# One hybrid layer on one core: the last plain tiles of the up projection are turned into Strassen steps

## The chip, the cores and the metric

The kernel runs on one core of one Trainium2 chip. The time is device time of one execution in microseconds; it is measured in several executions, and the median is given. A core has five engines with a queue each that is worked through strictly in order: TensorE (PE, with PEld for its weight loads), VectorE (DVE), ScalarE (ACT), GpSimd (POOL) and SyncE (SP). SP's queue only issues transfers between HBM and the on-chip memory. POOL's queue issues transfers too: here those that add what they bring to what is already there. An engine that waits for one instruction also holds back all that stand behind it.

## The reference

One layer of an encoder for 512 positions of width 1024, in float32. A recurrent group and an attention group are mixed into the residual stream; then follows the part that this change touches, the feed-forward block with 4096 hidden units:

```python
x = x + mix @ w_out[l]
h = rms_norm(x, mlp_norm_g[l])
x = x + jnp.square(jax.nn.relu(h @ w_up[l])) @ w_down[l]
return rms_norm(x, final_norm_g)
```

`h @ w_up` is a product of 512x1024 by 1024x4096, `... @ w_down` one of 512x4096 by 4096x1024. The row scale of the norm is applied after the down projection (relu squared lets a positive scale through as its square), so what the up projection reads is `x1n` turned on its side and scaled by the norm's gain, called `h2`.

## The kernel before

**Precision.** TensorE works on a rounded 32-bit type. So every operand is split into a high part (a rounded copy, made by ACT) and a low part (what the copy lost, made by DVE), and each product is three matmuls: high by high, high by low, low by high (`mm3`, lines 312 to 314). For a weight chunk of 128x1024 (512 KB) these parts are `whi` (`conv_hi`, line 247) and `wlo` (`conv_lo`, line 269). The chunks of the whole kernel stand in one list, `chunks`; while a step works on chunk c, its hook `feed` converts chunk c+3: ACT after the third of eight products, DVE after the fifth. There are four buffers each of `whi` and `wlo`, three of raw chunks (`wraw`) and four of chunks that are being summed (`tw`).

**The up projection** runs in two halves of 16 tiles of 128 hidden units. A plain tile (`n0` to `n3`) is 8 x 3 matmuls of 512 columns. Four tiles together, named by the first of them (0, 4, 8, 12), can instead be taken as a 2x2 block product in Strassen's way, with seven products in place of eight: the steps `11`, `t1`, `21`, `t2`, `22`, `t3`, `t4`, each 8 x 3 matmuls of 256 columns. A step multiplies a combination of weight blocks by a combination of quarters of `h2`. The weights of `11`, `21` and `22` are blocks as they lie in HBM, loaded into `wraw`. Those of the others are sums in `tw` buffers: t1 = 12+11, t2 = t1+22, t4 = t2+21, t3 = 12+22. A step converts its chunk, and then the same buffer becomes the next sum. The four sums of `h2` that belong to the steps t1, t2, t3 and 22 (`hsum`) are made by `h_sums`, split into `hh` and `hl`, and also written to HBM (`hsd`) for the second half. The `h2` quarters themselves come from eight transposes of four 128x128 blocks each (`h2_t`): TensorE turns `x1n` into `pxt`, ACT copies it out twice (`h2h`, the high part, and `hm`, the whole), DVE subtracts (`h2l`, by `h2_l`). The first four can be made while the output projection still runs; the other four need the last `x1n`.

The second half has always been four Strassen groups. The first half consists of the plain tiles 0 to 3 and the groups 4, 8 and 12. The plain tiles n0, n1 and n2 are the head: they take turns over the eight quarters of `h2`, and the transposes for quarters 4 to 7 stand in one piece after the first three products.

**Down projection.** After each half its 16 tiles go through the down projection, seven products of four chunks each (`dmm`), a step every 2.7 us of TensorE time. Its weights are loaded ahead, four of them (`ts`) with an add on POOL's queue.

**What sets the order.** ACT, DVE, POOL and TensorE run in the order in which the program is written. Extra work is hung on a place in it by the table `late`: (group, step, product) to a function. SP's queue is ordered by a scheduler, except in some stretches, where it too goes by the program.

Of the kernel before, what the change touches and what calls it, by code (L numbers as in the profile page):

```python
# [44 lines left out]
for _n, _w in (("w0", 4), ("w1", 4), ("w2", 4), ("w3", 4), ("cb", 4),  # L45
# [9 lines left out]
    "n0 n1 n2 4:11 4:t1 n3 4:t2 4:21 4:22 4:t3 8:11 8:t1 4:t4 8:21 8:t2 8:22 8:t3 12:11 12:t1 8:t4 12:t2 12:22 12:t3 12:21 12:t4",  # L55
    "0:11 0:t1 0:21 0:t2 0:22 0:t3 8:11 8:t1 0:t4 8:21 8:t2 8:22 8:t3 12:11 12:t1 8:t4 12:21 12:t2 12:22 12:t3 4:11 4:t1 12:t4 4:t2 4:22 4:t3 4:21 4:t4")
QUADS = ((4, 8, 12), (0, 8, 12, 4))
ON_ACT = {(h, f, k) for h in range(2) for f in QUADS[h] if (h, f) != (0, 4) for k in ("21", "22", "t3", "t4")}

# [5 lines left out]
def up_steps(h):  # L65
    return [("n", int(s[1:])) if s[0] == "n" else (s.split(":")[1], int(s.split(":")[0])) for s in STEPS[h].split()]
# [32 lines left out]
def hybrid_kernel(ctx: ExitStack, tc, xw0, xw, xn, w_in, w_v, w_out, w_up, w_dn, gates, vecs, bias, fg, out):  # L99
# [90 lines left out]
    cu, cq, cd_ = {}, {}, []  # L190
    for h in range(2):
        for kind, f0 in up_steps(h):
            if kind == "n":
                cu[h, f0] = len(chunks)
                chunks.append(w_up[h * HF + f0])
            else:
                cq[h, f0, kind] = len(chunks)
                chunks.append((h, kind, f0, "u"))
# [37 lines left out]
    for (h, f0, kind), i in cq.items():  # L236
        if kind == "11" and (h, f0) != (0, 4):
            swap[i], swap[i + 1] = i + 1, i
# [22 lines left out]
    def conv_lo(i):  # L261
        if i < len(chunks):
# [11 lines left out]
            if isinstance(c, tuple) and len(c) == 4:  # L274
# [4 lines left out]
                elif kind == "22":  # L279
                    t = raws[cq[h, f0, "t3"]]  # L280
                    nc.vector.tensor_tensor(t, t, r, op=OP.add)
                elif kind in ("t2", "21"):
# [896 lines left out]
    def load_t(half, n, f0):  # L1179
        t = work.tile([P, 1024], FT, name="tw", tag="tw", bufs=4)  # L1180
        nc.sync.dma_start(t, ublock(half, "12", f0))
        for b in {"t1": ("11",), "t2": ("11", "22"), "t3": ()}[n]:
            nc.gpsimd.dma_start(t, ublock(half, b, f0), accum_op=OP.add)
        raws[cq[half, f0, n]] = t

# [64 lines left out]
    BES["s1"].update({1: lambda: (o_lo("22", 0), o_lo("22", 1), h2_t(0, "gs")), 2: lambda: h2_t(1, "gs"), 3: lambda: (conv_lo(C_WA + 8), h2_l(0))})  # L1250
    BES["22"].update({1: lambda: (h2_t(2, "gs"), h2_l(1)), 2: lambda: (h2_t(3, "gs"), conv_lo(C_WA + 9)), 3: lambda: (h2_l(2), h2_l(3))})
    for w in OSEQ:
# [7 lines left out]
        if w in ("s3", "s4", "21"):  # L1260
            load_t(0, {"s3": "t1", "s4": "t2", "21": "t3"}[w], 4)
# [20 lines left out]

    def h2k(k):
        return (h2h[:, k, :], h2l[k])
# [29 lines left out]
    def up_evac(ff, p):  # L1314
        q, c = ff // 2, slice((ff % 2) * TH, (ff % 2 + 1) * TH)
        for t in range(2):
            if (q, t) not in rb:
                rb[q, t] = g_("a")
            act(rb[q, t][:, c], p[:, t * TH:(t + 1) * TH], AF.Relu)
        if ff % 2:  # L1320
            for t in range(2):
                nc.vector.tensor_tensor(rb[q, t], rb[q, t], rb[q, t], op=OP.mult)
                rb_done.add((q, t))
            up_pair(q)


# [5 lines left out]
    def h_sums(k):  # L1332
        m, c = k // 2, slice((k % 2) * TH, (k % 2 + 1) * TH)
        if k % 2 == 0:
            for n in SUMS:
                hsum[n, m] = g_("hsum")
        a, b = hm.pop(k), hm.pop(k + 4)
        e, s2, s3, s4 = [hsum[n, m][:, c] for n in SUMS]
        nc.vector.tensor_tensor(e, b[:, right], a[:, right], op=OP.subtract)
        stt(s2, a[:, left], -1.0, e, op0=OP.mult, op1=OP.subtract)  # L1340
        nc.vector.tensor_tensor(s3, a[:, left], a[:, right], op=OP.subtract)
        stt(s4, b[:, left], -1.0, s2, op0=OP.mult, op1=OP.subtract)
        if k % 2:
            for i, n in enumerate(SUMS):
                nc.sync.dma_start(hsd[i][:, m * S:(m + 1) * S], hsum[n, m])

    HSEQ = [(n, m) for n in ("t1", "t2", "22", "t3") for m in range(2)]
    HJ = 20
    FGP = ((0, 32, 64, 128), (0, 32, 64, 96, 128))
# [150 lines left out]
    def load_s1(half, ts, qs=range(NQ)):  # L1500
        for q in qs:
            t = ts[:, q, :]
            nc.sync.dma_start(t, wblock(half, "11", q))
            nc.gpsimd.dma_start(t, wblock(half, "12", q), accum_op=OP.add)
            raws[cd_[half] + 2 * q + 1] = t
# [9 lines left out]
    for half in range(2):  # L1515
        c0, cd = cu.get((half, 0)), cd_[half]
# [4 lines left out]
        start = 0  # L1521
        if half == 0:
            start = 3
            pu = [ps_("pu", "pj") for _ in range(start)]
            for k in range(KD):
                if k == 1:
                    for j in range(4, 8):
                        h2_t(j, "gs" if j < 6 else "et")
                        h2_l(j)
                for i in range(start):  # L1530
                    mm3(pu[i], wk(c0 + i, k), h2k(k), k == 0, k == KD - 1)
                    if i == 0:
                        feed(c0, k)
                if k in (2, 3, 4, 5):
                    h_sums(k - 2)
                if k == 6:
                    x1_sq(0, 0)
# [272 lines left out]
```

## Time and profile before

| | |
|---|---|
| median of 3 runs | 525.56 us (525.28 to 526.11) |
| profiled execution | 525.8 us, its span 524.0 us |
| up projection, first half | 200.78 to 284.87 us of the span |
| PE busy | 517.3 us (99%) |
| DVE, ACT, POOL busy | 430.3, 351.9, 65.8 us |
| DMA | 105.15 MB, mean 201 GB/s |

The page of the profile gives busy times, a picture of the span in 40 slices, the transfer queues, the chain of work that ended last and the costliest groups of instructions. Groups, waits and timelines can be had for a stretch of the span. "Busy" of a matmul counts its whole pipelined life, so matmuls overlap in it; how fast they follow one another is read from their start times. The three runs span 0.16%, so a change of about 0.2% is what a measurement can tell.

### The profile page before, as it was taken

How to read it: one execution, taken by the hardware profiler on the slowest of the kernel's cores; microseconds unless marked ns; L12 is line 12 of the kernel's file. 1: busy time of each engine (PE TensorE's matmuls, PEld its weight loads, DVE VectorE, ACT ScalarE, POOL GpSimd, SP SyncE). 2: the span in 40 equal slices, each digit the busy share in tenths (PEclk: the TensorE clock that was granted, in tenths of full speed). 3: DMA queues.
4: the chain of work that ended last, by engine and by line, in shares of the span. 5: the costliest groups of instructions: out<-in, count | busy, mean ns of one | idle time of the engine just before them, and what ended most of it. 6: DMA issues, size and time to landing. Idle time of an engine off the chain costs nothing.

```text
span 524.0 us, 8211 instructions
## 1 busy us (share of the span) xinstructions
PE 517.3 (99%) x3021; PEld 444.0 (85%) x3021; DVE 430.3 (82%) x668; ACT 351.9 (67%) x568; POOL 65.8 (13%) x90
## 2 busy tenths in 40 slices
PE   9999999999999999999999999999999999999995
PEld 8867888778787788899999888889999999888884
DVE  6899986788886898898789987789766978986985
ACT  7579946667855848585578666565667577655664
POOL 0173000000000321001300311001101300140000
PEclk9999999999999999999999999999999999999999
DMA  8636545367696499847595899976977497799804
GB/s 288 213 98 198 160 155 180 91 182 206 185 286 218 102 194 275 326 129 196 136 225 144 217 273 275 309 268 161 295 235 194 116 226 208 154 286 256 201 1 161
DMA packets 40329, 105.15 MB, mean 201 GB/s; under 512 B 5056, under 2 KB 13376, under 8 KB 40288
## 3 DMA queue, kind: packets, MB, share of 16 engines
q1 hardware_dynamic: 32448, 78.10, 44.7%
q0 software_dynamic: 7696, 26.32, 27.1%
q8 instruction: 24, 0.39, 0.3%
q10 hardware_dynamic: 144, 0.20, 0.1%
q14 instruction: 17, 0.14, 0.1%
HBM read 95.59 MB, written 4.29 MB: 191 GB/s over the span
## 4 chain that ended last, share of the span: by engine, by line
PE 96%; issue 2%; DVE 1%; POOL 1%; DVEq 0%; ACT 0%; POOLq 0%; ACTq 0%
PE pu L313 10%; PE pu L312 10%; PE pu L314 10%; PE pd L312 10%; PE pd L313 10%; PE pd L314 10%; PE pqk L312 3%; PE pqk L314 3%; PE pqk L313 3%; PE pwo L312 2%; PE pt L842 2%; PE pwo L314 2%; PE pwo L313 2%; PE ps L806 2%; PE pav L942 2%
## 5 line engine op out<-in xcount | busy, mean ns | idle before, releaser
L269 DVE TENSOR_TENSOR wlo<-wraw,whi 128x1024 fp32r<-128x1024 f32 x71 | 86.6, 1221 | 23.1 <-ACT whi L247 22.9
L247 ACT ACTIVATE whi<-wraw 128x1024 fp32r<-128x1024 f32 x67 | 70.8, 1058 | 37.5 <-PE pd L314 18.2
L313 PE MATMUL pd<-wlo,ah 128*128 128x512 f32 (+1 forms) x195 | 75.2, 386 | 0.0
L312 PE MATMUL pd<-whi,ah 128*128 128x512 f32 (+1 forms) x195 | 75.2, 386 | 0.0
L314 PE MATMUL pd<-whi,al 128*128 128x512 f32 (+1 forms) x195 | 75.2, 386 | 0.0
L314 PE MATMUL pu<-hh,wlo 128*128 128x256 f32 x224 | 63.4, 283 | 0.0
L313 PE MATMUL pu<-hl,whi 128*128 128x256 f32 x224 | 63.4, 283 | 0.0
L312 PE MATMUL pu<-hh,whi 128*128 128x256 f32 x224 | 63.4, 283 | 0.0
L269 DVE TENSOR_TENSOR wlo<-tw,whi 128x1024 fp32r<-128x1024 f32 x37 | 45.2, 1221 | 18.1 <-ACT whi L247 18.1
L312 PE MATMUL pu<-h2h,whi 128*128 128x256 f32 (+1 forms) x200 | 60.1, 300 | 0.0
L313 PE MATMUL pu<-h2l,whi 128*128 128x256 f32 (+1 forms) x200 | 60.0, 300 | 0.0
L314 PE MATMUL pu<-h2h,wlo 128*128 128x256 f32 (+1 forms) x200 | 60.0, 300 | 0.0
L247 ACT ACTIVATE whi<-tw 128x1024 fp32r<-128x1024 f32 x38 | 40.1, 1059 | 26.3 <-PE pd L314 6.3
L247 ACT ACTIVATE whi<-ts 128x1024 fp32r<-128x1024 f32 x24 | 25.5, 1061 | 26.3 <-PE pd L314 18.3
L312 PEld LDWEIGHTS pu<-hh,whi 128*128 128x128 f32 x224 | 43.0, 192 | 0.0
L313 PEld LDWEIGHTS pu<-hl,whi 128*128 128x128 f32 x224 | 43.0, 192 | 0.0
L314 PEld LDWEIGHTS pu<-hh,wlo 128*128 128x128 f32 x224 | 43.0, 192 | 0.0
L314 PEld LDWEIGHTS pd<-whi,al 128*128 128x128 f32 x195 | 36.6, 188 | 7.4
L312 PEld LDWEIGHTS pd<-whi,ah 128*128 128x128 f32 x195 | 36.6, 188 | 7.3
L313 PEld LDWEIGHTS pd<-wlo,ah 128*128 128x128 f32 x195 | 36.6, 188 | 7.3
L312 PEld LDWEIGHTS pu<-h2h,whi 128*128 128x128 f32 x200 | 38.3, 191 | 1.3
L314 PEld LDWEIGHTS pu<-h2h,wlo 128*128 128x128 f32 x200 | 38.3, 191 | 1.3
(277 smaller groups left out, 1219.8 us busy)
## 6 DMA issues: line engine op xcount, KB each, us to landing
wraw<-in_w_up_dram SPq DMA_DIRECT2D x25, 512.0 KB, 4.4
ts<-in_w_dn_dram POOLq DMA_DIRECT2D x24, 512.0 KB, 13.3
wraw<-in_w_dn_dram SPq DMA_DIRECT2D x24, 512.0 KB, 9.2
tw<-in_w_up_dram SPq DMA_DIRECT2D x15, 512.0 KB, 5.1
tw<-in_w_up_dram POOLq DMA_DIRECT2D x15, 512.0 KB, 8.3
wraw<-in_w_in_dram SPq DMA_DIRECT2D x13, 512.0 KB, 3.8
ts<-in_w_dn_dram SPq DMA_DIRECT2D x8, 512.0 KB, 6.8
tw<-in_w_dn_dram SPq DMA_DIRECT2D x8, 512.0 KB, 7.3
```

The costliest lines, as they stand in the source:

```text
L247: act(hi, raws[i], AF.Copy)
L269: nc.vector.tensor_tensor(lo, r, f(splits[i][0]), op=OP.subtract)
L312: nc.tensor.matmul(o, lhsT=a[0], rhs=b[0], start=bool(first), stop=False, skip_group_check=on)
L313: nc.tensor.matmul(o, lhsT=a[0], rhs=b[1], start=False, stop=False, skip_group_check=on)
L314: nc.tensor.matmul(o, lhsT=a[1], rhs=b[0], start=False, stop=bool(last), skip_group_check=on)
L806: nc.tensor.matmul(psq[p, u][e][:, :NK], lhsT=qs_[p, a][r, P * qt:P * qt + P], rhs=kks[p][r, b, w:w + NK], start=i == 0, stop=i == 2)
L842: nc.tensor.transpose(pt[:, i * P:(i + 1) * P], en[h][qt][:, k:k + P], ident)
L942: nc.tensor.matmul(pav[p][a, co], lhsT=vs[:, jt, h * DH:(h + 1) * DH], rhs=et[h, jt][:, ci], start=jt == 0 and i == 0, stop=jt == 3 and i ...
```

## The change

- The tiles 0 to 3 of the first half become a Strassen group too. The first half is now 28 steps: `0:11 8:11 4:11 0:21 8:21 4:21 0:t1 8:t1 0:t2 0:22 0:t3 8:t2 8:22 4:t1 0:t4 8:t3 4:t2 8:t4 4:22 12:11 4:t3 12:t1 4:t4 12:t2 12:22 12:t3 12:21 12:t4`.
- In the first step, 0:11, all products that read the high part of `h2` come first, those with the low part last. The transposes of quarters 4 and 5 stand in the middle of this step, those of 6 and 7 in the next one.
- The sums of `h2` are made one by one, ahead of their step (`h_sum`). Those for t1 and t2 stay with DVE. Those for t3 (four instructions) and for 22 (eight) go to POOL.
- More of the weight sums are made by adding transfers on POOL's queue: t3 of group 0, and t4 of all four groups, which DVE added before. t2 of group 0 is a load with two adds. DVE still adds t3 of groups 8, 4 and 12. The `21` results wait for a later step to be taken out of PSUM (`put`).
- Six of the eight row sums of squares (`x1_sq`) move into the down projection's first steps. One of seven small loads of the final gain at the end falls away.
- The squares of all groups are now ACT's (`ON_ACT`).
- From the ninth step on SP's queue of this half goes by the program. The first of the `ts` loads is issued in step 18 (8:t4), the load and the add of t1 of group 4 come in steps 5 and 6, and its step stands behind 8:22.

```diff
-    "n0 n1 n2 4:11 4:t1 n3 4:t2 4:21 4:22 4:t3 8:11 8:t1 4:t4 8:21 8:t2 8:22 8:t3 12:11 12:t1 8:t4 12:t2 12:22 12:t3 12:21 12:t4",
+    "0:11 8:11 4:11 0:21 8:21 4:21 0:t1 8:t1 0:t2 0:22 0:t3 8:t2 8:22 4:t1 0:t4 8:t3 4:t2 8:t4 4:22 12:11 4:t3 12:t1 4:t4 12:t2 12:22 12:t3 12:21 12:t4",
...
+AJ = {(0, 4), (1, 0)}
+ADDED = {(0, 0), (0, 12)}
+RAW = {(0, 0), (0, 4), (0, 8), (0, 12)}
+ON_ACT = {(h, f, k) for h in range(2) for f in QUADS[h] for k in ("21", "22", "t3", "t4")}
...
+                elif (h, f0) in RAW and kind == "t2":
+                    nc.gpsimd.dma_start(r, ublock(h, "21", f0), accum_op=OP.add)
+                    raws[cq[h, f0, "t4"]] = r
...
-        a, b = hm.pop(k), hm.pop(k + 4)
-        e, s2, s3, s4 = [hsum[n, m][:, c] for n in SUMS]
-        nc.vector.tensor_tensor(e, b[:, right], a[:, right], op=OP.subtract)
-        stt(s2, a[:, left], -1.0, e, op0=OP.mult, op1=OP.subtract)
-        nc.vector.tensor_tensor(s3, a[:, left], a[:, right], op=OP.subtract)
-        stt(s4, b[:, left], -1.0, s2, op0=OP.mult, op1=OP.subtract)
...
+        if n == "t1":
+            nc.vector.tensor_tensor(o, b[:, right], a[:, right], op=OP.subtract)
+        elif n == "t2":
+            stt(o, a[:, left], -1.0, hsr["t1", m][:, c], op0=OP.mult, op1=OP.subtract)
+        elif n == "t3":
+            nc.gpsimd.tensor_tensor(o, a[:, left], a[:, right], op=OP.subtract)
+        else:
+            nc.gpsimd.tensor_tensor(o, a[:, left], b[:, left], op=OP.subtract)
+            nc.gpsimd.tensor_tensor(o, o, hsr["t1", m][:, c], op=OP.add)
...
+                if head:
+                    nc.tensor.matmul(o, lhsT=w[0], rhs=x[0], start=first, stop=False, skip_group_check=True)
+                    nc.tensor.matmul(o, lhsT=w[1], rhs=x[0], start=False, stop=False, skip_group_check=True)
+                    for m in range(8) if n == 7 else ():
+                        nc.tensor.matmul(bank[b][:, m // 4 * TH:(m // 4 + 1) * TH], lhsT=hi[:, m * P:(m + 1) * P], rhs=h_part(kind, m % 4)[1],
...
+                         (0, "11", 1): sums(*[("t3", k) for k in range(4)]), (8, "11", 0): sums(("t1", 0), ("t1", 1)), (8, "11", 5): split_h("t1", 0),
+                         (4, "11", 0): sums(("t1", 2), ("t1", 3), ("22", 0), ("22", 1), ("22", 2), ("22", 3)),
+                         (4, "11", 1): split_h("t1", 1), (0, "21", 0): sums(("t2", 0), ("t2", 1)),
...
+            if half == 0 and j < 6:
+                x1_sq(1 + j // 2, j % 2)
```

The rest of the table `late`, which places the loads, adds and splits, is left out. How the order of instructions moves at the places that matter is shown for three queues. The line numbers of the changed kernel are up to 13 higher.

POOL, from the adds into the first `tw` sums (12+11 and so on) onward. Before:

```order
L1183 DMA tw<-in_w_up_dram 128x1024 x4
L277 DMA tw<-in_w_up_dram 128x1024
L1183 DMA tw<-in_w_up_dram 128x1024
L277 DMA tw<-in_w_up_dram 128x1024
L1504 DMA ts<-in_w_dn_dram 128x1024 x4
```

and after:

```order
L1196 DMA tw<-in_w_up_dram 128x1024 x4
L1338 TENSOR_TENSOR hsum<-hm 128x256 x4
L1196 DMA tw<-in_w_up_dram 128x1024
L1340 TENSOR_TENSOR hsum<-hm 128x256
L1341 TENSOR_TENSOR hsum<-hsum 128x256
L1340 TENSOR_TENSOR hsum<-hm 128x256
L1341 TENSOR_TENSOR hsum<-hsum 128x256
L1340 TENSOR_TENSOR hsum<-hm 128x256
L1341 TENSOR_TENSOR hsum<-hsum 128x256
L1340 TENSOR_TENSOR hsum<-hm 128x256
L1341 TENSOR_TENSOR hsum<-hsum 128x256
L278 DMA tw<-in_w_up_dram 128x1024
```

Twelve subtractions and additions of 128x256 stand between the adds now; in all there are 14 adds of up weights in this half, where there were 7.

DVE, from the last row block of the output projection (`x1n`) to the conversion of 4:21, the last `wlo` of the piece. After:

```order
L1218 SCALAR_TENSOR_TENSOR x1n<-pwo,nrc,x_1559 128x512
L270 TENSOR_TENSOR wlo<-wraw,whi 128x1024 x3
L1234 TENSOR_TENSOR h2l<-hm,h2h 128x512 x2
L1334 TENSOR_TENSOR hsum<-hm 128x256 x2
L1234 TENSOR_TENSOR h2l<-hm,h2h 128x512 x2
L270 TENSOR_TENSOR wlo<-wraw,whi 128x1024
L1362 TENSOR_TENSOR hl<-hsum,hh 128x512
L1334 TENSOR_TENSOR hsum<-hm 128x256 x2
L1362 TENSOR_TENSOR hl<-hsum,hh 128x512
L270 TENSOR_TENSOR wlo<-wraw,whi 128x1024
```

Before, from the same `x1n` on:

```order
L1206 SCALAR_TENSOR_TENSOR x1n<-pwo,nrc,x_1559 128x512
L1222 TENSOR_TENSOR h2l<-hm,h2h 128x512 x6
L1339 TENSOR_TENSOR hsum<-hm 128x256
L1340 SCALAR_TENSOR_TENSOR hsum<-hm,hsum 128x256
L1341 TENSOR_TENSOR hsum<-hm 128x256
L1342 SCALAR_TENSOR_TENSOR hsum<-hm,hsum 128x256
```

Five conversions of weights (8:11, 4:11, 0:21, 8:21, 4:21) now stand among the head's sums, where before none came until eight sums were made.

SP, behind the first loads of up weights; `hsd` are the writes of the sums to HBM. After:

```order
L1189 DMA tw<-in_w_up_dram 128x1024 x2
L229 DMA wraw<-in_w_up_dram 128x1024
L1343 DMA hsd_2266<-hsum 128x512 x2
L229 DMA wraw<-in_w_up_dram 128x1024 x3
L1343 DMA hsd_2264<-hsum 128x512
L229 DMA wraw<-in_w_up_dram 128x1024
```

Before:

```order
L1181 DMA tw<-in_w_up_dram 128x1024 x2
L230 DMA wraw<-in_w_up_dram 128x1024 x3
L1503 DMA ts<-in_w_dn_dram 128x1024 x4
L1345 DMA hsd_2269<-hsum 128x512
L1345 DMA hsd_2270<-hsum 128x512
```

The loads of 8:21, 4:21 and 0:22 (the three in a row) stand behind two writes that wait for POOL's first four sums; the four `ts` loads are gone from this place.

More of the change, by code (lines that the diff above doesn't have):

```diff
@@ L1312, in hybrid_kernel @@
     rb_done = set()
[L1314 to L1324, printed above, removed]
     SUMS = ("t1", "t2", "t3", "22")
@@ L1498, in fin_other, with load_s1, add_s1 @@
         nc.vector.tensor_tensor(xf[tt], x1n[tt, 1], fgt[1], op=OP.mult)
[L1500 to L1505, printed above, removed]
+    def load_s1(half, ts, q):
+        nc.sync.dma_start(ts[:, q, :], wblock(half, "11", q))
+    def add_s1(half, ts, q):
+        t = raws[cd_[half] + 2 * q + 1] = ts[:, q, :]
+        nc.gpsimd.dma_start(t, wblock(half, "12", q), accum_op=OP.add)
     def load_s3(half, q):
@@ L1515, in hybrid_kernel @@
     for half in range(2):
[L1516 removed]
+        cd = cd_[half]
         rb_done.clear()
@@ L1617, in hybrid_kernel @@
         qs = QUADS[half]
-        for f0, f1 in zip(qs, qs[1:]):
+        for f0, f1 in zip(qs, qs[1:]) if half else ():
             late[f0, "t2", 0] = lambda f1=f1: load_t(half, "t1", f1)
@@ L1702, in hybrid_kernel @@
                 load_s3(half, q)
+            if half == 0 and j < 4:
+                nr2[j] = consts.tile([P, 1], FT, name="nr2_%d" % j)
+            if half == 0 and j < 6:
+                x1_sq(1 + j // 2, j % 2)
+            if half == 0 and j == 6:
+                for tt in range(4):
+                    nc.vector.tensor_scalar(nr2[tt], r2[tt], -1.0, None, op0=OP.mult)
             if half == 0 and j == 16:
```

169 lines of the change are left out of this document (80 added, 89 removed).

## The prediction

> **What bounds the kernel now.** I read the page's busy times first.
>
> ```profile
> PE 517.3 (99%) x3021; PEld 444.0 (85%) x3021; DVE 430.3 (82%) x668; ACT 351.9 (67%) x568; POOL 65.8 (13%) x90
> ```
>
> TensorE is the bound: busy in 99% of the span. In the table by stage, the head (201 to 230 us), the Strassen groups (230 to 285) and the down projection (285 to 362) show no gap of it and the full clock (1.00):
>
> ```profile
> 201.00:230.00 29.00, 29.00 (x160) 25.13 (x159) 25.13 (x44) 19.96 (x37) 0.00 (x0) 1.00 0.81 274
> 230.00:285.00 55.00, 55.00 (x459) 54.96 (x458) 46.29 (x65) 36.38 (x54) 6.93 (x8) 1.00 0.67 167
> 285.00:362.00 77.00, 77.00 (x345) 63.88 (x344) 65.61 (x81) 48.52 (x64) 12.10 (x14) 1.00 0.92 252
> ```
>
> (Columns: stretch, its length, busy PE, PEld, DVE, ACT, POOL, each with its count, then clock, DMA share, GB/s.) So time can be won only by giving TensorE less to do, and is lost wherever it begins to wait. What it has to do is read from start times in its timeline:
>
> ```profile
> 200.78 0.40 PE L312 MATMUL pu<-h2h,whi 128*128 128x512 f32 x1
> ...
> 202.84 1.95 PE L1216 MATMUL pxt<-ident,x1n 128*128 128x128 f32 x16
> 204.54 0.48 PE L312 MATMUL pu<-h2h,whi 128*128 128x512 f32 x1
> ...
> 224.69 0.40 PE L312 MATMUL pu<-h2h,whi 128*128 128x512 f32 x1
> ...
> 230.15 0.28 PE L312 MATMUL pu<-hh,whi 128*128 128x256 f32 x1
> ...
> 233.03 0.28 PE L312 MATMUL pu<-h2h,whi 128*128 128x256 f32 x1
> ...
> 284.87 0.40 PE L312 MATMUL pd<-whi,ah 128*128 128x512 f32 x1
> ```
>
> A plain tile (n3) takes 230.15 - 224.69 = 5.46 us, a Strassen step (4:t2) 233.03 - 230.15 = 2.88, that is 0.12 per matmul; the 16 transposes take 204.54 - 202.84 = 1.70.
>
> **The change, part by part.**
>
> *TensorE.* Four plain tiles go (4 x 5.46 = 21.84), seven steps come (7 x 2.88 = 20.16): -1.7 us. The transposes stay, split in two. The first step only has its products in another order. Counting steps from 1, step n now starts at 200.78 + 1.70 + 2.88 (n - 1) from the third on: 4:21, the sixth, at 216.9.
>
> *Work of DVE and ACT over the whole stage.* These rows give the prices:
>
> ```profile
> L1222 DVE TENSOR_TENSOR h2l<-hm,h2h 128x512 fp32r<-128x512 f32 x7 | 4.7, 689 | 2.1 <-ACT hm L1219 2.1
> L269 DVE TENSOR_TENSOR wlo<-wraw,whi 128x1024 fp32r<-128x1024 f32 x2 | 2.4, 1220 | 0.0
> L1339 DVE TENSOR_TENSOR hsum<-hm 128x256 f32<-128x256 f32 x4 | 1.7, 418 | 0.0
> L1206 DVE SCALAR_TENSOR_TENSOR x1n<-pwo,nrc,x 128x512 f32<-128x512 f32 x2 | 1.5, 745 | 0.0
> L1363 DVE TENSOR_TENSOR hl<-hsum,hh 128x512 fp32r<-128x512 f32 x2 | 1.3, 688 | 0.0
> L286 DVE TENSOR_TENSOR tw<-tw,wraw 128x1024 f32<-128x1024 f32 x7 | 8.6, 1223 | 0.1
> ```
>
> ```profile
> L247 ACT ACTIVATE whi<-wraw 128x1024 fp32r<-128x1024 f32 x13 | 13.9, 1071 | 2.3 <-PE pu L313 1.6 <-ACT scr L1271 0.7
> L1219 ACT ACTIVATE hm<-pxt,vt 128x512 f32<-128x512 f32 x8 | 5.6, 701 | 0.0
> L1379 ACT ACTIVATE v<-pu 128x512 f32<-128x512 f32 x9 | 5.5, 606 | 6.3 <-PE pu L314 6.3
> L1360 ACT ACTIVATE hh<-hsum 128x512 fp32r<-128x512 f32 x8 | 5.3, 662 | 4.4 <-DVE hsum L1339 4.4
> L1271 ACT ACTIVATE scr<-x1n 128x512 f32<-128x512 f32 x8 | 5.0, 630 | 0.0
> ```
>
> DVE gets three conversions more (3 x 1.22) and three result sums (3 x 0.69), and loses three weight sums (3 x 1.22), eight of sixteen `h2` sums (8 x 0.42) and seven squares of plain tiles and group 4 (7 x 0.69): about 6 us less. ACT gets about 6 more: three `whi`, three copies `v`, the squares of groups 0 and 4, less the relus of the plain tiles and six sums of squares (0.83 each with their read). Both then have some 63 to 66 us of work in 82, so on the whole stage they hide: nothing. The six sums of squares go beside the down projection, where ACT has 48.5 of 77 us: nothing.
>
> *The head is where the cover is thin.* Before, three interleaved plain tiles gave DVE and ACT 16 us before a fourth chunk was needed. Now a chunk is needed every 2.88 us from the start. I walk DVE's queue to 4:21, its tightest place; neighbours overlap by 0.08. With POOL at no cost: transposes 4 and 5 at 202.5, the last `x1n` ready at 202.2, low part of 8:11 until 203.4. Only then is a buffer free for 8:21. Its load goes behind two writes of sums; a like load took 7.1 us in this stretch:
>
> ```profile
> wraw<-in_w_up_dram SPq DMA_DIRECT2D x3, 512.0 KB, 7.1
> ```
>
> It lands at 210.5, so its high part is ready at 211.6 and its low part at 212.8. DVE was done with the rest at about 209, so it waited. Then: `hl` of t1 until 213.4, two sums until 214.1, ACT's `hh` 214.7 and `whi` of 4:21 215.75, DVE's `wlo` 217.0. TensorE wants it with the third product of the step, 216.9 + 0.24 = 217.1. So it is just in time, and what POOL does decides.
>
> *POOL's twelve sums.* No row shows a 128x256 sum on POOL. The nearest:
>
> ```profile
> L163 POOL TENSOR_TENSOR pl<-pl,z 128x8 f32<-128x8 f32 x8 | 3.7, 463 | 0.7
> masks.py:199 POOL TENSOR_SCALAR_AFFINE_SELECT ident<-ident 128x128 f32<-128x128 f32 x1 | 0.3, 291 | 0.1
> L136 POOL MEMSET mhalf<- 128x4 f32 x1 | 0.1, 100 | 0.0
> ```
>
> An operation over 128 columns takes 0.29 with about 0.1 of it fixed (the fill of four columns takes that): 0.48 for 256. And DVE and POOL keep each other waiting. While DVE reads PSUM, a tiny POOL sum takes 0.20; while it subtracts two on-chip tiles, one takes 1.09 and ends as that subtraction ends:
>
> ```profile
> 29.58 0.20 POOL L163 TENSOR_TENSOR pl<-pl,z 128x8 f32<-128x8 f32 x1
> ```
>
> ```profile
> 29.36 1.28 DVE L496 TENSOR_TENSOR xr<-pxr,rrow 128x512 f32<-128x512 f32 x2
> ```
>
> ```profile
> 38.08 1.09 POOL L164 TENSOR_SCALAR pl<-pl 128x8 f32<-128x8 f32 x1
> ```
>
> ```profile
> 37.84 2.36 DVE L269 TENSOR_TENSOR wlo<-wraw,whi 128x1024 fp32r<-128x1024 f32 x2
> ```
>
> So I let the sums alternate with DVE's subtractions. At 0.48 the first four delay the last `x1n` by 0.6, to 202.8: the transposes wait 0.25. Of the eight for 22, five fall where DVE waits for 8:21 anyway, and the others push `wlo` of 4:21 from 217.0 to 217.7: 0.3 more of waiting. Together 0.55. Bounds: at 0.20 (the undisturbed row) nothing; at 1.09 each, five sums before 8:21 and four behind it put `wlo` of 4:21 at 222, some 5 us late, and the transposes about 1: 6 us. I take 0.48, since its row is nearest in size.
>
> The Trainium skill, SBUF — State Buffer, Who interferes with whom, has it that a VectorE instruction with two on-chip inputs and a GpSimd one that reads on-chip memory exclude each other for a whole instruction; the rows above agree. Its GPSIMD Engine Reference, section 3.1, gives 2.6 cycles per element for such a sum, which I estimate at 0.55 us for 256 columns; by it the waiting would be 1.2 in place of 0.55, and the time 525.1.
>
> *Transfers.* One load and seven adds more. The software queue carries the adds:
>
> ```profile
> q1 hardware_dynamic: 32448, 78.10, 44.7%
> q0 software_dynamic: 7696, 26.32, 27.1%
> ```
>
> (Packets, MB, share of 16 engines.) 27.1% of 524 us for 26.32 MB is 2.8 us of all engines per 512 KB add, so 20 us, and by the row above it 1.6 for the load. In 201 to 285 us the table by stage leaves 0.19 x 29 + 0.33 x 55 = 23.7 us idle, less 1.7: it fits, narrowly, and I cost it at nothing. The cover is the lead of three steps (8.6 us); if it goes, what is late next is the conversion that reads the sum.
>
> *The rest.* The small load saved at the end hides behind 80 us of down projection: nothing.
>
> **Sum.** Against the profiled execution, 525.8: -1.7 + 0.55 = 524.65. It lies 0.24 above the median, so by the median 525.56 - 1.15 = 524.4.
>
> **Rivals.**
>
> 1. *Full cover.* If POOL's sums take 0.3 or less, or the load of 8:21 lands a microsecond earlier, TensorE never waits: 525.56 - 1.7 = 523.9. For it: DVE has less work than before, with 4 us in hand in the head but for the wait on 8:21. Against it: no slack at 4:21.
> 2. *POOL holds DVE up longer (slower).* Each 0.1 us more per sum costs about 0.8 us, since eight or nine lie on the path; the gain is gone at about 0.62. At 0.7, `wlo` of 4:21 comes at 219.5, the waits are 2.4: 526.3. For it: the tiny sums beside subtractions already take 0.67 to 1.09. Against: that is mostly their waiting.
> 3. *Adds come late.* t2 of group 8 can only be added once DVE has converted 8:t1, at about 222 by the same walk, and two more adds are issued within 2 us. Alone an add lands in 6.1, in company it took up to 12.7:
>
> ```profile
> DMA to landing us min/median/max: 6.1/8.9/12.7
> ```
>
> At 12.7 it lands at 234.7, its two conversions end at 237.0, and 8:t2 wants them at 234.7: 2.3 lost, 526.7; with a second such place (12:t1, whose add is issued some 7 us before its conversion) 529. At the median of 8.9 nothing is lost.
>
> **Numbers.** Chances: forecast 0.45 (own range 523.9 to 525.2), full cover 0.16, POOL longer 0.21, adds late 0.13, other 0.05. 0.2%, about what a measurement of this kernel tells from no change, is 1.05 us, so faster means below 524.5: full cover and somewhat over half of the forecast, 0.42. Slower means above 526.6: adds late, the upper third of POOL longer, and the rest, 0.22. Same: 0.36. The range must leave out no more than 0.2: 523.8, just under full cover, to 526.8, which takes in rival 2 and one late add.
>
> **What would show it.** Right: the stage from the first `pu` to the first `pd` matmul lasts 82.4 + 0.55 us; the only PE waits in it are at the transposes and at 4:21; POOL's `hsum` rows take about 0.5. Rival 2: `hsum` rows on POOL of 0.7 or more, gaps between DVE's subtractions there, a wait of 2 us on `wlo` in the sixth step. Rival 3: ACT's `whi<-tw` waits for a transfer and PE for it, around 235 or 263 us. Wrong altogether: a wait of PE at a place not named here, or a down projection longer than before.

## The result, and the profile after

| | before | after |
|---|---|---|
| median | 525.45 us (525.28 to 526.16, 9 runs) | 526.87 us (526.11 to 528.18, 9 runs) |
| ratio | | 1.0028, 95% interval 1.0018 to 1.0039 |
| profiled execution, its span | 525.8, 524.0 us | 526.84, 525.1 us |
| first half, first `pu` to first `pd` matmul | 84.09 us | 85.65 us |
| first `pd` to last `pd` matmul | 233.00 us | 233.00 us |

The change makes the kernel 0.28% slower. All of it lies in the stage that was changed: +1.56 us in the profiled executions. (In the profiled execution of after this stage begins 0.56 us earlier: the kernel's first phase, which waits for its loads and which the change doesn't touch, was over sooner. That is why the spans differ by 1.1 only.) The page's busy times, and the same three stretches as in the prediction, now of the kernel after:

```profile
PE 515.9 (98%) x3093; PEld 445.7 (85%) x3093; DVE 428.3 (82%) x655; ACT 361.4 (69%) x581; POOL 85.2 (16%) x109
```

```profile
201.00:230.00 29.00, 26.63 (x222) 26.20 (x222) 26.04 (x35) 19.73 (x30) 14.29 (x13) 1.00 0.86 249
230.00:285.00 55.00, 54.90 (x457) 54.65 (x456) 41.42 (x50) 42.44 (x63) 9.38 (x11) 1.00 0.89 231
285.00:362.00 77.00, 77.00 (x345) 63.94 (x344) 65.75 (x92) 51.43 (x76) 12.09 (x14) 1.00 0.97 268
```

TensorE is busy 1.4 us less than before and yet the span is longer: it stands still for 2.4 us of the 29 in the head, where before it had no gap. The DMA share in the middle stretch rose from 0.67 to 0.89. TensorE's timeline shows where it stands:

```profile
200.22 0.28 PE L1547 MATMUL pu<-h2h,whi 128*128 128x256 f32 x1
...
201.89 0.27 PE L1228 MATMUL pxt<-ident,x1n 128*128 128x128 f32 x1
203.61 0.99 PE L1228 MATMUL pxt<-ident,x1n 128*128 128x128 f32 x7 [1.44 <-DVE x1n L1218]
...
218.13 0.28 PE L321 MATMUL pu<-h2l,whi 128*128 128x256 f32 x1
219.33 0.39 PE L322 MATMUL pu<-h2h,wlo 128*128 128x256 f32 x1 [0.92 <-DVE wlo L270]
...
253.63 0.28 PE L322 MATMUL pu<-hh,wlo 128*128 128x256 f32 x1
254.01 0.39 PE L320 MATMUL pu<-h2h,whi 128*128 128x256 f32 x1
...
285.87 0.40 PE L320 MATMUL pd<-whi,ah 128*128 128x512 f32 x1
```

Counted from start to start, against 0.12 us for a product and 0.11 for a transpose: 1.6 us lost at the transposes, 1.2 in 4:21 (with a slower restart), 0.4 at 254, where the step 8:t4 waits until the result of 8:t3 has been taken out of PSUM, and 0.1 at 268. That is 3.3, against 1.7 won.

Why the last `x1n` is late is seen by laying DVE's timeline beside POOL's. DVE:

```profile
197.44 3.59 DVE L1234 TENSOR_TENSOR h2l<-hm,h2h 128x512 fp32r<-128x512 f32 x2
200.95 0.74 DVE L1218 SCALAR_TENSOR_TENSOR x1n<-pwo,nrc,x 128x512 f32<-128x512 f32 x1
201.61 1.28 DVE L1234 TENSOR_TENSOR h2l<-hm,h2h 128x512 fp32r<-128x512 f32 x2
202.81 0.74 DVE L1218 SCALAR_TENSOR_TENSOR x1n<-pwo,nrc,x 128x512 f32<-128x512 f32 x1
```

and POOL, the four sums for t3 and the first for 22:

```profile
198.03 3.60 POOL L1338 TENSOR_TENSOR hsum<-hm 128x256 f32<-128x256 f32 x4
...
205.55 4.47 POOL L1340 TENSOR_TENSOR hsum<-hm 128x256 f32<-128x256 f32 x1 [3.10 <-ACT hm L1231]
```

Two low parts take 1.28 us at 201.6 and 3.59 at 197.4: 2.3 us longer, exactly while POOL works on its four sums. The second row of POOL shows the reverse. One sum takes 4.47 us. It ends at 210.0; with 0.74 us of its own, the shortest that a sum takes here, its turn came at about 209.3 (an estimate). DVE is at work without a pause, and at 209.4 it is through with all of these but the last:

```profile
204.60 2.35 DVE L270 TENSOR_TENSOR wlo<-wraw,whi 128x1024 fp32r<-128x1024 f32 x2
206.87 1.28 DVE L1234 TENSOR_TENSOR h2l<-hm,h2h 128x512 fp32r<-128x512 f32 x2
208.08 0.75 DVE L1334 TENSOR_TENSOR hsum<-hm 128x256 f32<-128x256 f32 x2
208.75 1.82 DVE L1234 TENSOR_TENSOR h2l<-hm,h2h 128x512 fp32r<-128x512 f32 x2
```

So there are two things to test: POOL's sums (theory A), and the added transfers (theory B), for which the DMA share speaks.

### The profile page after: what moved, and what is told of

Its sections match the earlier page's. It is cut to its first block, busy times and chain, and to the rows that moved or that the text cites. A ratio compares the mean times of both kernels' runs of the same rounds, so it can differ in the third digit from the quotient of the medians.

```text
span 525.1 us, 8396 instructions
## 1 busy us (share of the span) xinstructions
PE 515.9 (98%) x3093; PEld 445.7 (85%) x3093; DVE 428.3 (82%) x655; ACT 361.4 (69%) x581; POOL 85.2 (16%) x109
## 4 chain that ended last, share of the span: by engine, by line
PE 85%; DMA 5%; DVE 4%; issue 3%; ACT 1%; POOL 1%; DVEq 0%; POOLq 0%; ACTq 0%
PE pd L320 10%; PE pd L321 10%; PE pd L322 10%; PE pu L320 7%; PE pu L321 7%; PE pu L322 7%; DMA tw<-in_w_up_dram 4%; PE pqk L320 3%; PE pqk L322 3%; PE pqk L321 3%; PE pt L850 2%; PE ps L814 2%; PE pwo L320 2%; PE pwo L322 2%; PE pwo L321 2%
## 5 line engine op out<-in xcount | busy, mean ns | idle before, releaser
L320 PE MATMUL pu<-hh,whi 128*128 128x256 f32 x256 | 72.4, 283 | 0.0
L321 PE MATMUL pu<-hl,whi 128*128 128x256 f32 x256 | 72.4, 283 | 0.0
L322 PE MATMUL pu<-hh,wlo 128*128 128x256 f32 x256 | 72.4, 283 | 0.0
L322 PE MATMUL pu<-h2h,wlo 128*128 128x256 f32 x184 | 52.2, 283 | 0.9 <-DVE wlo L270 0.9
L320 PE MATMUL pu<-h2h,whi 128*128 128x256 f32 x184 | 52.3, 284 | 0.1
L321 PE MATMUL pu<-h2l,whi 128*128 128x256 f32 x184 | 52.0, 283 | 0.0
L320 PEld LDWEIGHTS pu<-hh,whi 128*128 128x128 f32 x256 | 49.2, 192 | 0.0
L321 PEld LDWEIGHTS pu<-hl,whi 128*128 128x128 f32 x256 | 49.2, 192 | 0.0
L322 PEld LDWEIGHTS pu<-hh,wlo 128*128 128x128 f32 x256 | 49.2, 192 | 0.0
L270 DVE TENSOR_TENSOR wlo<-ts,whi 128x1024 fp32r<-128x1024 f32 x24 | 29.3, 1222 | 8.9 <-ACT whi L248 8.6
```

The lines of the kernel that those rows point to most:

```text
L270: nc.vector.tensor_tensor(lo, r, f(splits[i][0]), op=OP.subtract)
L320: nc.tensor.matmul(o, lhsT=a[0], rhs=b[0], start=bool(first), stop=False, skip_group_check=on)
L321: nc.tensor.matmul(o, lhsT=a[0], rhs=b[1], start=False, stop=False, skip_group_check=on)
L322: nc.tensor.matmul(o, lhsT=a[1], rhs=b[0], start=False, stop=bool(last), skip_group_check=on)
```

## The experiments

Each was timed beside the kernel before on the same chip, whose medians there were 525.4 to 525.55 us. "Ratio" is to that kernel, from all executions together; it can differ from the quotient of the two medians by up to 0.14%.

| kernel | edit, from the changed kernel | median us | ratio, 95% interval |
|---|---|---|---|
| changed | | 526.87 | 1.0028 (1.0018 to 1.0039) |
| e1 | t3 sums on DVE | 526.82 | 1.0026 (1.0016 to 1.0037) |
| e2 | 22 sums on DVE | 528.17 | 1.0067 (1.0044 to 1.0091) |
| e3 | both on DVE | 527.39 | 1.0042 (1.0026 to 1.0059) |
| e4 | two low parts behind the last `x1n` | 527.65 | 1.0042 (1.0027 to 1.0058) |
| f1 | e3, two adds left out | 523.91 | 0.9976 (0.9965 to 0.9988) |
| f2 | e3, t3 sum of group 8 later | 525.34 | 1.0001 (0.9989 to 1.0012) |
| f3 | e3, that and two more things later | 524.61 | 0.9991 (0.9978 to 1.0004) |
| f4 | f3's later places, all sums on POOL | 527.50 | 1.0035 (1.0022 to 1.0048) |
| g1 | f3, t3 sums on POOL | 526.85 | 1.0027 (1.0016 to 1.0037) |
| g2 | f3, 22 sums on POOL | 525.96 | 1.0004 (0.9995 to 1.0013) |
| g3 | f3, one add replaced by a load | 528.68 | 1.0054 (1.0037 to 1.0071) |
| g4 | changed, two adds left out | 526.59 | 1.0023 (1.0013 to 1.0033) |
| h3 | f3, DVE's last sums still later | 525.48 | 0.9991 (0.9982 to 1.0000) |
| h5 | f3, the same, some earlier | 524.52 | 0.9992 (0.9978 to 1.0007) |

### e1, e2, e3: POOL's sums taken away

The edit of e1, and that of e2; e3 is both:

```diff
-            nc.gpsimd.tensor_tensor(o, a[:, left], a[:, right], op=OP.subtract)
+            nc.vector.tensor_tensor(o, a[:, left], a[:, right], op=OP.subtract)
...
-                         (0, "11", 1): sums(*[("t3", k) for k in range(4)]),
+                         (8, "11", 2): sums(*[("t3", k) for k in range(4)]),
```

```diff
-            nc.gpsimd.tensor_tensor(o, a[:, left], b[:, left], op=OP.subtract)
-            nc.gpsimd.tensor_tensor(o, o, hsr["t1", m][:, c], op=OP.add)
+            stt(o, b[:, left], -1.0, hsr["t2", m][:, c],
+                op0=OP.mult, op1=OP.subtract)
...
-                         (4, "11", 0): sums(("t1", 2), ("t1", 3), ("22", 0), ("22", 1), ("22", 2), ("22", 3)),
+                         (4, "11", 0): sums(("t1", 2), ("t1", 3)), (4, "21", 1): sums(*[("22", k) for k in range(4)]),
```

> The four sums of h2 for t3 are made by DVE in place of POOL, ahead of the low part of 8:21, where DVE sat idle for 2.1 us in the changed kernel's trace. Theory A (POOL's sums hold DVE up: a low part of h2 that takes 0.68 us elsewhere took 2.99 beside these four): the last x1n comes about 2.3 us earlier, so the wait of 1.6 us at the transposes goes; the buffer for 8:21 comes free 2.3 us earlier, and of the 1.1 us of waiting in 4:21 at most 0.3 is left, since TensorE wants that chunk 1.6 us earlier too: 526.9 - 2.4 = 524.5. Theory B (the transfers are what is late: one more load, seven more adds): the first wait goes, but 8:21 lands as late as before and 4:21 waits by as much more: 526.9. Nothing gained at all would mean that x1n waited for something else than POOL.

Measured 526.82: nothing gained. TensorE's waits in e1 (engine, tile and line, what it waited for, us in total, times, longest):

```profile
PE pu L322 <- DVE wlo L270: 1.4, 1, 1.4
PE pu L320 <- DVE a L1388: 0.8, 1, 0.8
```

The wait at the transposes is gone, as A said. But 4:21 waits 1.4 us in place of 0.9, since the eight sums for 22 now hold DVE up on their own (g2, below, against f3 shows it), and a wait of 0.8 appears at 268. A's forecast of what is left in 4:21 (0.3) was wrong.

> The eight POOL sums for 22 are replaced by four on DVE (22 = -b - t2, 0.34 us each), behind those for t2. Those for t3 stay on POOL. Theory A: in the stretch from 205 to 219 us four DVE instructions took 2.0 us more than they take elsewhere, all of it beside these sums. Without them 4:21 waits for nothing (1.1 us less), the transposes still wait 1.6 us: 525.8, if the 1.4 us more of DVE's own work in steps 6 and 7 is hidden; DVE is nearly full there (217 to 230 us), so up to 1 us may come back: 525.8 to 526.8. Theory B: the load of 8:21 lands at 211.5 as before and sets 4:21: 526.9.

Measured 528.17, more than either theory gave. In its profile 4:21 no longer waits, the transposes wait 2.5 us from start to start, and the result of 8:t3 is waited for by 0.9 at 254. The transposes wait longer than in the changed kernel because the low part beside POOL's sums takes 3.84 us here: all four sums go through before it, where in the changed kernel three did. The profiled execution took 527.37; what the median has above it is not traced.

> Both edits: POOL makes no sum of h2 at all. Theory A: both waits go and only the 0.4 us at 254 and the few tenths of restarts stay: 526.9 - 1.6 - 1.1 = 524.2, that is 1.3 below the kernel of before. Theory B: no change, 526.9, with PE waiting for a conversion behind a late transfer. If the sum of the two single edits' gains is larger than this one's, they share a cause: the one DVE chain that ends at 4:21.

Measured 527.39. Without any sum on POOL the head is nearly free of waits (0.45 us at 216, none at the transposes), and the kernel is no faster. The time is lost again 25 us later. DVE's timeline of e3 there:

```profile
231.63 1.23 DVE L270 TENSOR_TENSOR wlo<-wraw,whi 128x1024 fp32r<-128x1024 f32 x1 [0.21 <-ACT whi L248]
238.15 1.23 DVE L282 TENSOR_TENSOR tw<-tw,wraw 128x1024 f32<-128x1024 f32 x1 [5.29 <-DMA tw<-in_w_up_dram]
239.29 1.28 DVE L1388 TENSOR_TENSOR a<-v,pu 128x512 f32<-128x512 f32 x2
240.49 1.22 DVE L270 TENSOR_TENSOR wlo<-tw,whi 128x1024 fp32r<-128x1024 f32 x1
```

DVE is to add block 22 of group 8 to its t3 buffer (L282) and waits 5.3 us for that buffer's load. Behind it in the queue stand two results that free PSUM (L1388), and `wlo` of 4:t1. TensorE waits for both, 0.6 and 1.3 us. So theory A accounts for the head, and something on the side of the transfers takes the gain back.

### e4: only DVE's order

```diff
-    BES["22"].update({0: lambda: h2_l(1), 1: lambda: (h2_t(3, "gs"), h2_l(2)), 2: lambda: (h2_l(3), conv_hi(C_WA + 9)), 3: lambda: None})
+    BES["22"].update({0: lambda: h2_l(1), 1: lambda: h2_t(3, "gs"), 2: lambda: conv_hi(C_WA + 9), 3: lambda: (h2_l(2), h2_l(3))})
```

> Only DVE's order is changed: the two low parts of h2 that stand between the last two x1n go behind the last one, nothing leaves POOL. The last x1n then comes 1.28 us earlier, and the wait at the transposes falls from 1.6 to 0.3. Theory A with one chain on DVE: the conversion of 8:11 comes no earlier (it stands behind the same work), so the buffer for 8:21 and with it 4:21 come as late as before, and the 1.28 us are waited for again in 4:21: 526.9, with the wait there at about 2.3. Rival: the waits are two separate ones, and the first is won outright: 525.6.

Measured 527.65. Nothing was won. The waits of its profiled execution (530.8, near the top of its runs, 526.2 to 531.4):

```profile
PE pu L322 <- DVE wlo L270: 2.4, 2, 1.4
PE pu L320 <- DVE a L1388: 1.7, 2, 0.9
PE pxt L1228 <- DVE x1n L1218: 0.8, 2, 0.4
```

The transposes wait less, `wlo` of 4:21 is waited for by 1.4 us in place of 0.9, and the late waits are there besides. It fits the one chain on DVE (`wlo` of 8:11, buffer, load of 8:21, `wlo` of 8:21, `wlo` of 4:21), but with so much else in this execution it doesn't prove it.

### f1 and g4: two adds left out

Both leave out the two adding transfers that make t4 of groups 0 and 8, and with them that part of the computation; f1 from e3, g4 from the changed kernel itself:

```diff
-                    nc.gpsimd.dma_start(r, ublock(h, "21", f0), accum_op=OP.add)
+                    if f0 not in (0, 8):
+                        nc.gpsimd.dma_start(r, ublock(h, "21", f0), accum_op=OP.add)
```

> As e3 (no sum on POOL), and the adds that make t4 of groups 0 and 8 are left out, two of the 14 adds of up weights in this half: those two steps multiply t2's weights, so this kernel leaves that part of the computation out. In e3's trace DVE waits 5.3 us (232.9 to 238.2) for the load of t3 of group 8 while three adds are under way and the DMA engines are 99% busy; behind it stand the result sums and the low part that TensorE then waits for, 2.0 us, and a slower clock for some 16 matmuls after that, 1.5 us more. Theory B (the added transfers fill the DMA engines): without the two adds that load lands 3 us or more earlier, and the 3.5 us go; the wait of 0.9 at 269 stays: about 524.6. Rival (the load is late because its buffer comes free late, at 227.9): the wait at 240 stays, 527 to 528.

Measured 523.91, 3.5 below e3. TensorE waits nowhere in the stage; start and end of it in the timeline of f1:

```profile
200.33 0.28 PE L1548 MATMUL pu<-h2h,whi 128*128 128x256 f32 x1
...
282.69 0.40 PE L321 MATMUL pd<-whi,ah 128*128 128x512 f32 x1
```

82.36 us, 1.7 less than before. The load of t3 of group 8 is waited for by 2.4 us only, and DVE's sum is done 4.3 us earlier than in e3:

```profile
233.85 1.22 DVE L282 TENSOR_TENSOR tw<-tw,wraw 128x1024 f32<-128x1024 f32 x1 [2.39 <-DMA tw<-in_w_up_dram]
```

The load is issued at 226.8 in place of 227.9, and from there to DVE's sum it takes 7.1 us in place of 10.2. So of the 4.3 us at most 1.2 come from a buffer that is free earlier (the rival), and 3.1 from the transfer itself.

> The changed kernel with POOL's sums as they are, but without the adds that make t4 of groups 0 and 8 (those two steps multiply t2's weights; that part of the computation is left out). With e3 (527.4) and f1 (523.9) it completes the square of POOL's sums and adds. If each causes waits of its own, this one loses only the 0.5 us at 254 and 268: 526.4, and the two causes hide each other: taking one away alone gains under 0.5, taking both 3.0. If the adds alone set the time, 523.9.

Measured 526.59, as expected: the waits of the head are all there in g4, and nothing behind them.

```profile
PE pxt L1229 <- DVE x1n L1219: 1.3, 1, 1.3
PE pu L323 <- DVE wlo L270: 0.8, 1, 0.8
```

The four kernels make a square:

| median us | with all adds | two adds left out |
|---|---|---|
| sums on POOL | 526.87 | 526.59 |
| sums on DVE | 527.39 | 523.91 |

Taking away one cause gains -0.5 or 0.3 us, taking away both 3.0. Each hides behind the other: as long as POOL makes the head 2.8 us late, the late transfers find a TensorE that is late too. The traces show it: in the changed kernel DVE's sum for t3 of group 8 starts at 237.9, hardly sooner than in e3 (238.15), and `wlo` of 4:t1 is done at 241.4. But TensorE comes to 4:t1 only at 242.2 there, and in e3 it wanted to go on at 239.5.

How crowded the transfers are is seen in the stretch from 225 to 235 us, by queue (packets, MB, share of the 16 engines), and in how long they took to land (KB each, median us). Before:

```profile
q1 hardware_dynamic: 305, 1.07, 33.5%
...
wraw<-in_w_up_dram SPq DMA_DIRECT2D x2, 512.0 KB, 3.6
```

and after:

```profile
q0 software_dynamic: 338, 1.26, 71.1%
q1 hardware_dynamic: 342, 1.05, 30.3%
...
tw<-in_w_up_dram POOLq DMA_DIRECT2D x3, 512.0 KB, 8.6
wraw<-in_w_up_dram SPq DMA_DIRECT2D x1, 512.0 KB, 6.6
```

Before, no add was under way in this stretch and a third of the engines' time was used. Now the adds alone take 71%, and a plain load takes 6.6 us in place of 3.6.

### f2, f3, f4: nothing behind the late load

f2 leaves every transfer as it is and moves DVE's sum for t3 of group 8 behind what TensorE needs sooner. f3 does so for group 4 too, and doesn't take up the sums for the down projection in steps 20 to 22. f4 has these later places, with all sums on POOL. The edit is shown as f3 has it; f2 has `(8,)` in place of `(8, 4)`, only the first of the two later places, and not the last change.

```diff
-                    nc.vector.tensor_tensor(t, t, r, op=OP.add)
+                    if h == 0 and f0 in (8, 4):
+                        st["t3", f0] = (t, r)
+                    else:
+                        nc.vector.tensor_tensor(t, t, r, op=OP.add)
...
+            late.update({(8, "t2", 5): t3_sum(8), (4, "t2", 0): t3_sum(4),
...
-                if n in (5, 7):
+                if n in (5, 7) and not 20 <= st["step"] <= 22:
                     op_next()
```

(`t3_sum(f0)` makes the sum that was put aside.)

> As e3, but DVE's sum for t3 of group 8 stands 1.5 steps later, behind the low parts of 4:t1 and 0:t4. No transfer is changed. If what hurts at 240 is that DVE's queue stands still behind one late load (queue theory), the result sums and the low part of 4:t1 come at 235 to 237 and the 3.5 us go, though the transfers are as late as before: about 524.6, the 0.9 at 269 stays. If the transfers themselves are too late for TensorE (plain theory B), the wait moves to 0:t4 or 8:t3 with 1 us or more: 526 or more.

Measured 525.34, 2.1 below e3. DVE's timeline of f2 at the same place:

```profile
235.68 1.23 DVE L270 TENSOR_TENSOR wlo<-tw,whi 128x1024 fp32r<-128x1024 f32 x1 [1.23 <-ACT whi L248]
...
240.63 1.22 DVE L1608 TENSOR_TENSOR tw<-tw,wraw 128x1024 f32<-128x1024 f32 x1
```

`wlo` of 4:t1 starts at 235.7 in place of 240.5, and TensorE has no wait at 240. So it was the queue behind the load, and not the adds themselves, that TensorE waited for there. The waits at 254 and 268 are left (1.2 and 1.0 us in its profile), and one of 0.9 in 4:21. That profiled execution took 527.14, 1.8 above the median, so the places are read from it, and not their sizes.

> As the one before, and the same for group 4 (its t3 sum behind the result sum of 8:t3), and the hidden results' sums for the down projection are not taken up in steps 20 to 22, where DVE has no pause (261 to 273.6 us in the changed kernel's trace) and TensorE waits for the result of 4:t3. Queue theory: every wait seen so far but 0.4 at 217 is gone, the stage lasts 28 x 2.88 + 1.9 for the transposes + 0.6 = 83.2 us against 84.1 in the kernel before: 524.6 at most, 523.9 if the wait at 217 goes too. If DVE is simply short of time between 260 and 285, the wait comes back later, at the first chunks of the down projection, and the gain over the one before is nothing.

Measured 524.61, 2.3 below the changed kernel and on the verge of beating the kernel before (its interval reaches 1.0004). Its profiled stage is 82.97 us, with one wait left, for the result of 12:t3 at 280:

```profile
PE pu L323 <- DVE a L1391: 0.4, 1, 0.4
```

> The changed kernel with the same later places on DVE, but POOL keeps its twelve sums. Theory A and the queue theory together: the 1.5 us at the transposes and the 1.1 in 4:21 stay, the 0.5 us at 254 and 268 go: 526.4, and against the one before the difference is what POOL's sums cost, about 2 us. If POOL's sums cost nothing once the later places are free, it is as fast as the one before.

Measured 527.50: with POOL's sums the later places gain nothing. f4 and f3 differ in POOL's sums alone: 2.9 us.

### g1, g2: which of POOL's sums

Each is f3 with one of e3's two edits taken back.

> f3 (all sums on DVE, later places) with one edit taken back: the four sums for t3 are POOL's again, in the first step. If POOL keeps DVE out for as long as its own instructions follow one another, the last x1n comes 2.3 us later as in the changed kernel, the transposes wait 1.5 to 2.4 us and a few tenths are added in 4:21: 524.6 + 2.0 = 526.6. If the two engines take turns, as the prediction had it, the wait is 0.25: 524.9.

> f3 with only the eight sums for 22 back on POOL, in the third step. In e1, where they were alone on POOL, TensorE waited 1.7 us in 4:21: 524.6 + 1.7 = 526.3. If only sums beside the last x1n matter, 524.6.

Measured 526.85 and 525.96: +2.2 us for the four sums in the first step, +1.4 for the eight in the third (2.9 for all twelve). Each makes the one wait that A names, first g1, then g2:

```profile
PE pxt L1231 <- DVE x1n L1221: 1.4, 1, 1.4
```

```profile
PE pu L325 <- DVE wlo L270: 1.4, 1, 1.4
```

That is the price of POOL's sums, place by place. For g1 it holds between the medians only: its profiled execution took 525.57, 1.3 less than its median, and its stage is 1.0 us longer than f3's (83.97 and 82.97). At the transposes the two engines don't take turns as the prediction had it (0.25): in g1, too, three of POOL's sums go through before the low part issued beside them is done. But between 207 and 212 us of g2 they do take turns. DVE's two low parts there take 2.37 us in place of 1.28, some 0.55 more for each, while POOL's sums end one by one:

```profile
208.14 2.37 DVE L1237 TENSOR_TENSOR h2l<-hm,h2h 128x512 fp32r<-128x512 f32 x2
```

```profile
208.77 1.18 POOL L1343 TENSOR_TENSOR hsum<-hm 128x256 f32<-128x256 f32 x1
210.03 1.07 POOL L1344 TENSOR_TENSOR hsum<-hsum 128x256 f32<-128x256 f32 x1
```

So how many instructions of the one go ahead of the other isn't fixed: one, three or four sums, or some six of DVE's instructions. What decides it, these runs don't show.

### g3, h3, h5: attempts at the rest

g3 makes t4 of group 8 on DVE, from a second load of block 21, which takes the place of the load of 12:11:

```diff
+                elif (h, f0, kind) == (0, 8, "t2"):
+                    raws[cq[h, f0, "t4"]] = r
...
+                if (h, f0, kind) == (0, 8, "22"):
+                    st["x"] = stream.tile([P, 1024], FT, name="wraw", tag="wraw", bufs=3)
+                    nc.sync.dma_start(st["x"], ublock(0, "21", 8))
```

> f3 with one add less: t4 of group 8 is made by DVE from a second load of its block 21 on SP's queue (the load of 12:11 moves back behind it). An add costs 2.8 us of all DMA engines, a load 1.6; the load takes the place of one that stood in the crowded stretch from 225 to 238 us, so 2.8 us go there. DVE has 1.2 us more to do at 238 to 241, where it waited. If the crowded transfers are what is left (f1, which left two adds out, had no wait at all at 523.9), 524.0, and the higher ones of its runs come down. If f3 has nothing left that hangs on transfers: 524.6.

Measured 528.68. The trace, of an execution of 526.75, shows one reason; what the median has above that is not traced. The load goes into a buffer that comes free only with DVE's sum for t3 of group 8 at 240, and DVE waits for it with everything else behind:

```profile
238.83 1.22 DVE L1613 TENSOR_TENSOR tw<-tw,wraw 128x1024 f32<-128x1024 f32 x1
243.47 1.23 DVE L1620 TENSOR_TENSOR tw<-tw,wraw 128x1024 f32<-128x1024 f32 x1 [3.42 <-DMA wraw<-in_w_up_dram]
```

The edit built the very wait that f2 had taken away, so it says nothing on what one add less would bring.

h3 and h5 hold DVE's sums for the down projection back at the end of the stage too:

```diff
-                if n in (5, 7) and not 20 <= st["step"] <= 22:
+                if n in (5, 7) and st["step"] not in (20, 21, 22, 26, 27):
```

(h5: 20, 21, 26 and 27.)

> f3, and DVE's sums for the down projection are taken up in neither of the steps 26 and 27 either (in f3 they stand ahead of the result sum of 12:t3, for which TensorE waits 0.6 us at 280). If the rest in f3 is DVE's order: stage 82.4, 524.0. If it is transfers: 524.6. Left for later, these sums (four more of 0.69) could make the first low parts of the down projection late: then TensorE waits just behind 283 us, 524.6 or more.

> The same, but those sums are taken up in step 22 again, where DVE is idle for 2.1 us in f3's trace (264.4 to 266.5), so that fewer are left for the end. DVE's order: 524.0 or a little below the one before. If step 22 has no room for them, the wait at 268 of the changed kernel is back with up to 1 us: 525.

Measured 525.48 and 524.52, with the same ratio as f3. What f3 has left above f1 (0.7 us) doesn't go away with the order of these sums: in h3 waits of 0.9, 0.3 and 1.2 us come at 269, 275 and 282 in its profiled execution (526.03, above its median). That it goes when two adds are left out points to the transfers; a kernel that computes everything without these adds was not found, so it isn't shown.

## Why the prediction was wrong

It said 524.4 (523.8 to 526.8); 526.87 was measured. By its own steps:

- **TensorE, -1.7 us: right.** f1, which has all 28 steps and no wait, takes 82.36 us in the stage; the prediction had 82.4.
- **The rest of DVE's and ACT's work, nothing: right as a sum, wrong at one place.** Over the stage both have time left. But DVE's queue is in order, and in e3 it stood still for 5.3 us while work that TensorE needed stood behind.
- **POOL's twelve sums, 0.55 us: the step that failed.** Two things were wrong in it. The price: 0.48 us was taken from the nearest row; the shortest sum on POOL takes 0.74, the four for t3 take 0.9 each by their row. And the way the two engines meet: the prediction let them alternate and had the last `x1n` 0.6 us late, a figure that it doesn't work out. In the trace the second low part, issued with POOL's first sum at 198.0, is done at 201.0, when three of four sums are through: 2.99 us in place of 0.68. The sum at 205.5 in its turn waits for some six of DVE's instructions. Counted from the first `pu` matmul the last `x1n` is done after 3.3 us, in e1 after 1.5: 1.9 late. Measured: 2.8 us of waiting in the changed kernel (1.6 at the transposes, where 0.25 was forecast, and 1.2 in 4:21, where 0.3 was), 2.9 between f4 and f3.
- **Where it would wait: right for all but 0.5 us.** The transposes and 4:21 were named; the second has its reason in the buffer for 8:21, as walked. In the trace the load of 8:21 is issued at 204.8, when `wlo` of 8:11 is done, and its high part begins at 211.6 instead of 210.5. The losses at 254 (0.4, for a result still in PSUM) and 268 (0.1) were not named, and the prediction itself had a wait at another place as a sign of being wrong.
- **Rival 2 is close to what happened**: 0.7 per sum, 2.4 us late in all, 526.3. It had 0.21. But it reached 2.4 with sums that alternate, and looked for 2 us of waiting in the sixth step; 1.2 were there, and 1.6 had come at the transposes before. So that its time is so near is in part luck. The rows that spoke for it (0.67 to 1.09 for tiny sums beside subtractions) were set aside as "mostly their waiting"; but waiting for each other was the cost to be estimated.
- **Transfers, "fits narrowly, nothing": failed too**, though it shows only behind the first. Over the stage they did fit (mean shares 0.86 and 0.89). But the adds are not spread over the stage; four of them are issued between 223.8 and 233.2, and from 225 to 235 the share reaches 1.0. Once POOL is out of the way, two adds fewer are worth 3.5 us (e3 against f1). Rival 3 had a price (2.3 us) and a place (about 235) near what e3 shows at 240; what came too late for TensorE was not the added t2, but a plain load beside the adds, and what DVE had queued behind it.
- **Six sums of squares and the small load, nothing: right.** From the first to the last `pd` matmul it is 233.00 us in both, and behind that 6.2 us in both.

The Trainium skill, SBUF — State Buffer, Who interferes with whom, says of VectorE's 2-port modes that whoever issues first has the shared ports "for the whole instruction" and that the other one blocks; an instruction with two on-chip inputs, as here, contends with GpSimd's reads. The trace agrees that one blocks, but here a low part waited for three sums (2.99 us), and a sum for some six instructions of DVE (4.47 us). Its GPSIMD Engine Reference, section 3.1, from which the prediction estimated 0.55 us a sum, is below what was measured (0.74).

What stays open: what decides whether POOL or DVE goes on; and why the runs of most kernels with the new order spread over 2 to 5 us, where those of the kernel before stay within 1.9.

## What to carry to other kernels

Work handed to an idle POOL isn't free for a DVE that subtracts on-chip tiles at the same time. Price it as if several of POOL's instructions go ahead of one of DVE's (here three or four), and put it where DVE waits for something else, or leave it on DVE: here four sums of 0.42 us on DVE cost less than the same four on POOL. Check transfers by the stretch in which they are issued, not by the stage's mean, and ask of each instruction that waits for one what stands behind it in the queue. When two causes hide each other, taking one away shows nothing; only the square of both told them apart.

## What the runs showed of the hardware

**Two short waits were followed by a slower clock, in one trace.** After the waits of 0.6 and 1.3 us in e3, TensorE's matmuls followed each other more slowly for 3.4 us. The granted clock in e3's table of stretches (the column behind POOL's) fell from 1.00 to 0.88:

```profile
225.00:235.00 10.00, 10.00 (x86) 10.00 (x85) 5.96 (x7) 6.06 (x10) 1.80 (x3) 1.00 0.99 244
235.00:245.00 10.00, 8.36 (x59) 7.98 (x58) 6.78 (x11) 6.21 (x11) 0.85 (x1) 0.88 0.73 167
```

In TensorE's timeline the distance from start to start goes from 0.12 to 0.21 us, and back at 246:

```profile
240.12 0.35 PE L320 MATMUL pu<-hh,whi 128*128 128x256 f32 x1 [0.48 <-DVE a L1388]
240.31 0.28 PE L321 MATMUL pu<-hl,whi 128*128 128x256 f32 x1
241.76 0.38 PE L322 MATMUL pu<-hh,wlo 128*128 128x256 f32 x1 [1.17 <-DVE wlo L270]
...
243.01 0.42 PE L321 MATMUL pu<-hl,whi 128*128 128x256 f32 x1
243.22 0.41 PE L322 MATMUL pu<-hh,wlo 128*128 128x256 f32 x1
...
245.99 0.28 PE L320 MATMUL pu<-h2h,whi 128*128 128x256 f32 x1
```

16 matmuls lost some 1.5 us that way, nearly as much as the waits themselves. The wait of 1.6 us at the transposes in the changed kernel was not followed by it. The Trainium skill, TensorE: Matmul & The Clock Gate, Part 1, has the clock fall to half after an idle window of about 3.4 us. Here it came after 2.0 us of waiting within 2.4 us, less than that; that the slow stretch lasts 3.4 us agrees with such a window. It doesn't follow each time: 0.8 and 1.7 us of waiting within 2.8 us at the transposes of f4 had no such effect. So that the waits brought it on is not shown, nor what decides it.
